# Attention outputs stored as two halves and added in the gating step, in a two-layer streaming encoder

## The chip, the cores and the metric

The kernel runs on one NeuronCore of a Trainium2 chip. Five engines work side by side: TensorE (PE) for matmuls, VectorE (DVE), ScalarE (ACT) and GpSimd (POOL) for element-wise work, and SyncE (SP), which here issues every DMA. Matmuls write to PSUM; the other operands lie in SBUF; the large intermediates go through DRAM. The metric is the device time of one execution in microseconds (us), the median of several runs.

## The reference

The program is one inference step of two encoder layers for 2048 prompt tokens and 32 sample tokens, with d_model 1024. What matters here is layer 0: two attention branches from one projection, each gated, concatenated and sent through one output projection.

```python
qa, ka, va, ga, qb, kb, vb, gb = ab_project(hp, pos_p, w_in_ab[j])
oa = prompt_band(qa, ka, va, N_PREV_A, None, sinks_a[j])      # 8 query heads, 2 KV heads, window 2 chunks, sinks
ob = prompt_band(qb, kb, vb, N_PREV_B, relpos_b[j], None)     # 8 heads, window 8 chunks, bias table
mp = ab_output(oa, ob, ga, gb, w_out_ab[j])

def ab_output(oa, ob, ga, gb, w_out):
    y = jnp.concatenate([oa.reshape(b, t, -1) * jax.nn.silu(ga),
                         ob.reshape(b, t, -1) * jax.nn.silu(gb)], axis=-1)
    return y @ w_out
```

Layer 1 is a gated linear recurrence (projection, width-4 convolution, gates, scan, output projection). Everything is fp32.

## The kernel before, in words

**Precision.** A matrix product in fp32 is made of fast products of a high and a low part: each operand is split into h (rounded) and l (the rest), and three matmuls h·h, h·l, l·h are summed in PSUM (`mm_list`, L819). So every weight tile is split (`w_split`, L484: the copy h on ACT or DVE, the difference l on DVE or POOL), and every activation block too (`r0h`, `r0l`). In the attention the values v lie as 64 high and 64 low columns side by side, so one matmul gives 128 PSUM rows: rows 0 to 63 from the high part of v, rows 64 to 127 from its low part. Their sum is the attention output of a head.

**Stages.** Tokens are cut into three blocks b of about 700, each in two halves bi of 352 (the last 324). `dense_P` (L1126) runs the 26 column tiles of the input projection for b = 0, 1, 2. As soon as q, k and v of a block have been written to DRAM, the attention units of that block start. `dense_2` (L1954) then runs the output projection (`out_part`) of the three blocks, and layer 1 block by block.

**One attention unit** (`soft`, L1231, and `transp`, `evac_O`, `evac_B`). PE makes the scores S. `reduce` (L1242) runs one custom DVE operation per PSUM tile: it adds bias or mask, writes the negated scores to `pt` and their row minimum to `nm`. Branch B has its keys in two PSUM tiles, so two operations give two minima, and a third small operation `nm<-nm` (L1257) joins them. ACT takes the exponential with the row sum; DVE takes the reciprocal `rr`; DVE or POOL scales `pt` by `rr` and by 0.5 (the 0.5 belongs to the gate, which is stored as twice its SiLU). PE transposes the result into T; ACT and DVE split T into the two parts `pp`. PE multiplies by v into O.

**Evacuation of O.** `evac_O` (branch A, four heads side by side, 512 columns) lets ACT copy one 64-row half of O to the tile `ot`, and DVE add the other half. `evac_B` (branch B) has 512 columns in which the high and low part of the scores lie beside each other too, so that a second DVE operation adds `ot` to `ot` over 256 columns. One DMA then writes 64 rows to oT in DRAM, which has 1024 rows, one per output feature.

**Gating.** `y_proc` (L784) loads oT and the gate zT in pieces of 4 feature tiles by 176 tokens, multiplies them, and splits the product into `r0h`/`r0l` (or `r1h`/`r1l`), the operand of the output projection. For block 0 it starts near the end of `dense_P`, and writes over `r0` once `dense_P` no longer reads it.

**What sets the order.** The instructions of every engine are put in order while the program is built, by a list scheduler (`Sched`): each step is a small process that waits for its inputs and buffers, states its cost on each engine it may use, and gets the engine that would end first. PE never waits in that plan: matmuls of the dense parts, four at a time (`CHK`), fill what the attention leaves free. After the attention `sch.alone` keeps POOL out of such choices. On the chip each engine runs its list strictly in that order, and waits on semaphores. So a change of a cost or a step moves instructions in all lists.

## Time and profile before

| what | value |
|---|---|
| median of 3 runs | 1827.37 us (1827.22 to 1828.31) |
| the profiled execution | 1823.5 us |
| its span, first to last instruction | 1821.7 us |
| mean granted TensorE clock | 0.988 |
| DMA, moved | 362.80 MB, mean 199 GB/s |
| attention, first and last O matmul start | 95.3 us, about 1002 us |

The profile was taken by the hardware profiler on one execution. Nearly every instruction is issued through one helper, so that all rows have the line L101; groups are told apart by the tiles that they write and read, written as out<-in. "CUSTOM_DVE_ANT_0 pt<-S,bias" is the operation of `reduce`, and "DVE_READ_ACCUMULATOR2_ANT nm" the read of its minimum. A row of a group gives its count after x, then busy time and mean ns of one, then the idle time of the engine just before them with what ended it. A row of the stages gives start:end, length, and for each engine its busy us, then the granted clock, the DMA share and GB/s. Records of one matmul are longer than the distance between two starts, because matmuls overlap.

### The profile page before, as it was taken

How to read it: one execution, taken by the hardware profiler on the slowest of the kernel's cores; microseconds unless marked ns; L12 is line 12 of the kernel's file. 1: busy time of each engine (PE TensorE's matmuls, PEld its weight loads, DVE VectorE, ACT ScalarE, POOL GpSimd, SP SyncE). 2: the span in 40 equal slices, each digit the busy share in tenths (PEclk: the TensorE clock that was granted, in tenths of full speed). 3: DMA queues.
4: the chain of work that ended last, by engine and by line, in shares of the span. 5: the costliest groups of instructions: out<-in, count | busy, mean ns of one | idle time of the engine just before them, and what ended most of it. 6: DMA issues, size and time to landing. Idle time of an engine off the chain costs nothing.

```text
span 1821.7 us, 31694 instructions
## 1 busy us (share of the span) xinstructions
PE 1731.5 (95%) x11078; PEld 1671.8 (92%) x11078; DVE 1555.3 (85%) x3330; ACT 996.5 (55%) x2037; POOL 326.5 (18%) x284
## 2 busy tenths in 40 slices
PE   8999999999999999999998999998999999999995
PEld 7999999998999999899997999998999899999995
DVE  9899967899998779998988789899999988798843
ACT  4275543476666416665565344457753675447831
POOL 4332204323322233311222000000011000100002
PEclk8999999999999999999998999999999999999998
DMA  5788766888654368877764985684566735575376
GB/s 179 203 245 265 228 190 196 226 232 237 192 149 141 97 186 248 210 217 195 216 194 122 278 248 168 210 267 147 217 213 217 204 124 174 165 208 171 128 268 193
DMA packets 293576, 362.80 MB, mean 199 GB/s; under 512 B 36308, under 2 KB 244616, under 8 KB 293400
## 3 DMA queue, kind: packets, MB, share of 16 engines
q1 hardware_dynamic: 293416, 360.78, 66.5%
q8 instruction: 87, 1.43, 0.3%
q14 instruction: 73, 0.60, 0.1%
HBM read 255.77 MB, written 107.00 MB: 199 GB/s over the span
## 4 chain that ended last, share of the span: by engine, by line
PE 49%; DVE 29%; DMA 9%; ACT 6%; issue 4%; SPq 1%; POOL 1%; DVEq 0%; ACTq 0%; POOLq 0%
PE acc L101 35%; PE T L101 4%; PE O L101 4%; PE S L101 4%; DVE pt L101 3%; DVE ex L101 3%; DVE m L101 3%; DMA xr<-x2T 3%; DVE ss L101 2%; DVE ti L101 2%; DVE xs L101 2%; DVE s L101 2%; DVE pp L101 2%; DVE eti L101 1%; DVE wl L101 1%
## 5 line engine op out<-in xcount | busy, mean ns | idle before, releaser
L101 PE MATMUL acc<-r0h,wh 128*128 128x352 f32 (+2 forms) x1832 | 592.1, 323 | 6.7 <-ACT tzb L101 2.9
L101 PE MATMUL acc<-r0h,wl 128*128 128x352 f32 (+2 forms) x1832 | 592.2, 323 | 2.9 <-DMA wl<-wo1s 2.9
L101 PE MATMUL acc<-r0l,wh 128*128 128x352 f32 (+2 forms) x1832 | 592.5, 323 | 0.6 <-DVE r0l L101 0.5
L101 PEld LDWEIGHTS acc<-r0h,wh 128*128 128x128 f32 x1832 | 346.2, 189 | 9.3 <-ACT tzb L101 3.1
L101 PEld LDWEIGHTS acc<-r0h,wl 128*128 128x128 f32 x1832 | 346.3, 189 | 4.8 <-DMA wl<-wo1s 4.0
L101 PEld LDWEIGHTS acc<-r0l,wh 128*128 128x128 f32 x1832 | 346.4, 189 | 2.2 <-DVE r0l L101 1.2
L101 PE MATMUL acc<-r1h,wh 128*128 128x352 f32 (+1 forms) x864 | 277.5, 321 | 5.2 <-ACT tz L101 3.6
L101 PE MATMUL acc<-r1h,wl 128*128 128x352 f32 (+1 forms) x864 | 277.0, 321 | 1.6 <-DVE wl L101 1.6
L101 PE MATMUL acc<-r1l,wh 128*128 128x352 f32 (+1 forms) x864 | 276.9, 321 | 0.0
L101 ACT ACTIVATE pt<-pt,nm 128x256 f32<-128x256 f32 (+6 forms) x272 | 169.8, 627 | 61.2 <-DVE nm L101 59.3
L101 ACT CAST pp<-T 128x256 fp32r<-128x256 f32 (+4 forms) x314 | 134.0, 438 | 84.3 <-PE T L101 65.8
L101 PEld LDWEIGHTS acc<-r1h,wh 128*128 128x128 f32 x864 | 162.3, 188 | 6.4 <-ACT tz L101 4.5
L101 POOL TENSOR_SCALAR pt<-pt,rr 128x256 f32<-128x256 f32 (+4 forms) x142 | 100.2, 716 | 366.4 <-DVE rr L101 217.0
L101 PEld LDWEIGHTS acc<-r1h,wl 128*128 128x128 f32 x864 | 162.3, 188 | 1.9 <-DVE wl L101 1.9
L101 PEld LDWEIGHTS acc<-r1l,wh 128*128 128x128 f32 x864 | 162.3, 188 | 0.0
L101 PE MATMUL T<-ident,pt 128*128 128x128 f32 (+2 forms) x864 | 143.3, 274 | 18.0 <-DVE pp L101 10.2
L101 DVE TENSOR_TENSOR pp<-T,pp 128x256 fp32r<-128x256 f32 (+4 forms) x314 | 150.4, 496 | 7.9 <-ACT pp L101 6.0
L101 PE MATMUL O<-pp,vt 128*128 128x256 f32 (+3 forms) x728 | 135.9, 310 | 9.8 <-DVE pp L101 4.7
L101 PEld LDWEIGHTS T<-ident,pt 128*128 128x128 f32 (+2 forms) x864 | 101.7, 140 | 42.4 <-DVE pp L101 19.9
L101 DVE CUSTOM_DVE_ANT_0 pt<-S,bias 128x320 f32<-128x320 f32 (+2 forms) x240 | 108.8, 478 | 17.4 <-PE S L101 14.6
L101 PE MATMUL S<-kk,qa 128*128 128x320 f32 (+5 forms) x376 | 119.7, 333 | 3.8 <-DVE nm L101 3.3
L101 PEld LDWEIGHTS O<-pp,vt 128*128 128x128 f32 (+1 forms) x728 | 107.1, 193 | 16.0 <-DVE pp L101 6.1
(241 smaller groups left out, 3010.1 us busy)
## 6 DMA issues: line engine op xcount, KB each, us to landing
wst<-w_in SPq DMA_DIRECT2D x93, 512.0 KB, 4.4
wst<-wo_in SPq DMA_DIRECT2D x32, 512.0 KB, 5.6
wh<-w1s SPq DMA_DIRECT2D x32, 512.0 KB, 3.8
wl<-w1s SPq DMA_DIRECT2D x32, 512.0 KB, 4.6
wh<-wo1s SPq DMA_DIRECT2D x24, 512.0 KB, 3.9
wl<-wo1s SPq DMA_DIRECT2D x24, 512.0 KB, 4.7
kk<-kB SPq DMA_DIRECT2D x32, 320.0 KB, 4.8
vt<-vB SPq DMA_DIRECT2D x16, 640.0 KB, 4.8
```

What stands on the lines that cost most here:

```text
L101: r = fn(*a, **k)
```

## The change

- oT gets 2048 rows. For each head the sums from the high and from the low half of v are both kept; they are added when the gating step reads them.
- Branch A (`evac_O`): two ACT copies of 128 rows by 256 columns and two DMAs; no DVE operation. The ring `ot` is four tiles of 256 columns instead of four half-tiles of 512.
- Branch B and the sample units (`evac_add`): ACT copies one 256-column part over all 128 rows, DVE adds the other part; the second DVE addition is gone.
- `y_proc`: pieces of 2 feature tiles by 352 tokens. Two DMAs bring the high rows and the low rows, z comes in one tile for two pieces. One more addition per piece, then product, copy and difference as before. The readiness of the operand is told for each feature tile (`(key, bi, c)`), no longer for the whole half.
- `reduce`: the minimum of the first PSUM tile is the start value of the second operation, and the small `nm<-nm` is gone.
- The scaling of `pt` may go to ACT for branch B (units with one row of `out`), and no longer has the factor 0.5; the 24 weight tiles of the output projection are multiplied by 0.5 in `w_split` instead, where their difference l is now always on DVE.

```diff
-    oT, zT, x2T = dt("oT", [D, TOK]), dt("zT", [D, TOK]), dt("x2T", [D, TOK])
+    oT, zT, x2T = dt("oT", [2 * D, TOK]), dt("zT", [D, TOK]), dt("x2T", [D, TOK])
...
+            half = WSEQ[i][0] == "wo0"
+            if half:
+                if e == "A":
+                    A.activation(h, s, AF.Copy, scale=0.5)
+                else:
+                    V.tensor_scalar(h, s, 0.5, None, OP.mult)
+                yield R("V", [h])
+                V.scalar_tensor_tensor(l, s, 0.5, f32(h), OP.mult, OP.subtract)
...
     def y_proc(b, ri, key, free=None, then=None):
-        todo = [(bi, t0, col, w, 4 * j) for bi, t0, col, w in cells_of(b) for j in range(2)]
+        todo = [(bi, T0[2 * b + bi], BW[2 * b + bi], k) for bi in range(2) for k in range(0, KT, 2)]
...
+                if k % 4 == 0:
+                    g = xrr if b == 0 else xtr
+                    z, = yield R("SP", [("z", b)], [g])
+                    SP.dma_start(out=tile4(z)[:, :, :w], in_=zT[k * 128:k * 128 + 512, t0:t0 + w].rearrange("(k p) t -> p k t", p=128))
+                x, = yield R("SP", [("o", min(b + 1, 2))], [xtr])
+                for j in range(2):
+                    r = k * 256 + j * 256
+                    SP.dma_start(out=tile4(x)[j * 64:j * 64 + 64, :, :w], in_=oT[r:r + 256, t0:t0 + w].rearrange("(s d) t -> d s t", s=4))
...
-            ENG[e].tensor_tensor(o, o, x[:, 4:8, :w], OP.mult)
+            ENG[e].tensor_tensor(o, o, v[:, :, 1], OP.add)
+            e, _ = yield R(("V", "G"), [lambda: th, z], cost=(0.8, 1.63))
+            ENG[e].tensor_tensor(o, o, tile4(z)[:, k % 4:k % 4 + 2, :w], OP.mult)
...
-            if n % 4 == 3:
-                sch.set((key, bi), max(sch.t["V"], sch.t["G"]) + 0.13)
+            for c in range(k, k + 2):
+                sch.set((key, bi, c), sch.t[e] + 0.13)
...
-    otr = Ring(sch, ap, [128, 512], F32, "ot", 2, halves=True)
+    otr = ring(ap, [128, 256], "ot", 4)
...
-        def reduce(ps, pieces, o0):
-            yield R("V", [ps] + ex)
+        def reduce(ps, pieces, o0, gi):
+            on = gi > 0 and sink is None
+            yield R("V", [ps] + ex + ([(uid, 0)] if on else []))
...
-                                       scalar=BIG if sink is None else nsk[:np_, sink + j:sink + j + 1],
+                                       scalar=nsk[:np_, sink + j:sink + j + 1] if sink is not None else nm[:np_, 1:2] if on else BIG,
...
-                if sink is None and len(groups) == 2:
-                    V.tensor_tensor(nm[:np_, 0:1], nm[:np_, 0:1], nm[:np_, 1:2], OP.min)
...
-        e, _ = yield R(("V", "G"), [r], cost=(0.06 + n * 0.00053, 0.1 + n * 0.00106))
+        e, _ = yield R(("V", "G", "A")[:3 if len(out) == 1 else 2], [r], cost=(0.06 + n * 0.00053, 0.1 + n * 0.00106, 0.197 + n / 1200.0))
...
-            ENG[e].tensor_scalar(x, x, r[:np_, j:j + 1], 0.5, OP.mult, OP.mult)
+            if e == "A":
+                A.activation(x, x, AF.Copy, scale=r[:np_, j:j + 1])
+            else:
+                ENG[e].tensor_scalar(x, x, r[:np_, j:j + 1], None, OP.mult)
...
+    def evac_O(b, ps, g, t0):
+        for i in range(2):
+            ot, = yield R("A", [ps], [otr])
+            A.copy(ot, ps[:, i * 256:i * 256 + 256])
+            if i:
+                Or.release(ps)
+            yield R("SP", [ot])
+            SP.dma_start(out=o_two(g, i, t0, 128), in_=ot.rearrange("p (j n) -> p j n", j=2))
+            otr.release(ot)
+        o_done(b)
...
+    def evac_add(b, ps, v0, v1, dsts, i0=None):
...
+            A.copy(o2[:, i0:], v0[:, i0:])
+            if i0:
+                A.copy(o2[:, 0], v1[:, 0])
+            yield R("V", [ot])
+            V.tensor_tensor(o2[:, i0:], v1[:, i0:], o2[:, i0:], OP.add)
         Or.release(ps)
...
-    def evac_B(b, ps, dst, i0):
-        A.copy(o[:, i0:], v[64 - x:128 - x, i0:])
-        V.tensor_tensor(o[:, i0:], v[x:x + 64, i0:], o[:, i0:], OP.add)
-        V.tensor_tensor(o[:, i0:, 1], o[:, i0:, 0], o[:, i0:, 1], OP.add)
-        SP.dma_start(out=dst, in_=ot[:, 256:512])
```

All lists move. Three places are shown; the numbers behind a tile's name tell its buffers apart.

The first place is DVE in the last attention units of branch B, where O is emptied (`ot`), T is split (`pp`) and the minimum is taken (`pt`, `nm`). Before:

```order
L101 TENSOR_TENSOR ot_215<-O_198,ot_215 64x2x2x128
L101 TENSOR_TENSOR pp_213<-T_196,pp_213 128x3x128
L101 ISA pt_211,nm_218<-S_194,bias_208 128x320
L101 ISA nm_218 128x1
L101 TENSOR_TENSOR ot_215<-ot_215 64x256
L101 TENSOR_TENSOR pp_213<-T_197,pp_213 128x2x128
L101 ISA pt_211,nm_218<-S_195,bias_208 128x320
L101 ISA nm_218 128x1
L101 TENSOR_TENSOR nm_218<-nm_218 128x1
```

and now:

```order
L101 ISA pt_209,nm_218<-S_194,bias_208 128x320
L101 ISA nm_218 128x1
L101 ISA pt_209,nm_218<-S_195,bias_208,nm_218 128x320
L101 ISA nm_218 128x1
L101 TENSOR_TENSOR pp_213<-T_196,pp_213 32x32
L101 TENSOR_TENSOR ot_216<-O_198,ot_216 128x256
```

The join `nm<-nm` and the addition `ot<-ot` are gone, the addition of O has 256 columns over 128 rows, and the second custom operation reads `nm`.

The second place is DVE where the attention ends and the operand of the first output projection (`r0l`, from `xt`) is made. Before, this is mixed with attention units:

```order
L101 TENSOR_TENSOR xt_152<-xt_152 128x704
L101 TENSOR_TENSOR pp_212<-T_196,pp_212 128x4x32
L101 TENSOR_TENSOR ot_214<-O_198,ot_214 64x2x2x128
L101 ISA pt_210,nm_217<-S_194,bias_207 32x272
L101 ISA nm_217 32x1
L101 TENSOR_TENSOR r0l<-xt_152,r0h 128x4x176
```

and now it stands behind the last split `pp` of the attention, between weight splits (`wh`, `wl`) and the last gates (`s`):

```order
L101 TENSOR_TENSOR pp_213<-T_197,pp_213 128x2x128
L101 TENSOR_TENSOR r0l<-xt_151,r0h 128x2x352
L101 TENSOR_TENSOR r0l<-xt_152,r0h 128x2x352
L101 TENSOR_TENSOR ot_215<-O_198,ot_215 128x256
L101 SCALAR_TENSOR_TENSOR s_187<-s_187,acc_158 128x352
L101 TENSOR_SCALAR wh_119<-wst_117 128x1024
L101 SCALAR_TENSOR_TENSOR wl_122<-wst_117,wh_119 128x1024
L101 SCALAR_TENSOR_TENSOR s_182<-s_182,acc_159 128x324
L101 TENSOR_TENSOR xt_151<-xt_151 128x2x352
L101 TENSOR_SCALAR wh_120<-wst_118 128x1024
L101 TENSOR_TENSOR xt_151<-xt_151,xr_153 128x2x352
```

So the gating of block 0 moved from the attention's last units to behind them.

The third place is PE at the last O matmuls. Before, what follows is the output projection (352 columns, block 0):

```order
L101 MATMUL O_198<-pp_212,vt_206 128x2x128 x8
L101 MATMUL O_198<-pp_212,vt_206 128x256 x2
L101 MATMUL acc_159<-r0h,wl_123 128x352
L101 MATMUL acc_159<-r0h,wh_120 128x352
L101 MATMUL acc_159<-r0l,wh_120 128x352
```

and now it is the end of the input projection (the 324 columns are the last half of block 2; the last O matmul stands one row above):

```order
L101 MATMUL acc_158<-r0h,wh_121 128x352
L101 MATMUL acc_158<-r0l,wh_121 128x352
L101 MATMUL acc_158<-r0h,wl_124 128x352
L101 MATMUL acc_159<-r0h,wh_119 128x324
L101 MATMUL acc_159<-r0l,wh_119 128x324
L101 MATMUL acc_159<-r0h,wl_122 128x324
```

What filled PE inside the attention now follows it. Counted over the whole list of PE, 168 dense matmuls moved from ahead of the last O matmul to behind it: between it and the first matmul on `r1` there are now 460 dense matmuls, where there were 292. 76 of them still belong to the input projection. The number of matmuls is the same, 11061. Over the whole list of DVE there are 3183 instructions, where there were 3332, on ACT 1836 (1767), on POOL 199 (289), and on SP 1274 (1227); of the 142 scalings of `pt` on POOL 69 are left, 44 stand on ACT (none before), and DVE has 159 (130).

More of the change, by code (lines that the diff above doesn't have):

```diff
@@ L566, in late_consts @@
         V.tensor_scalar(nsk, sk, -1.0, None, OP.mult)
-        SP.dma_start(out=oT[:, SEQ:S0].rearrange("(k p) t -> p k t", p=128), in_=zpad)
+        for x in range(2):
+            SP.dma_start(out=oT[x * D:(x + 1) * D, SEQ:S0].rearrange("(k p) t -> p k t", p=128), in_=zpad)
         V.tensor_scalar(hba, vec[:, BA], 0.5, None, OP.mult)
@@ L1410, in proc @@
                 run.v_done(2)
[L1411 removed]
+                yield from evac_add(b, po, out[:, :, 0], out[:, :, 1], [o_head(8 + h, ta * 128, 256)], 2 - len(edges))
             return proc
@@ L1509, in proc @@
             run.v_done()
-            yield from evac_O(2, po, 128, oT[g * 256:(g + 1) * 256, S0:TOK].rearrange("(j d) n -> d j n", j=4),
-                              lambda ot: ot[:, :128].rearrange("d (j n) -> d j n", j=4), True)
+            yield from evac_add(2, po, po[:, 128:256], po[:, :128], [o_two(g, i, S0, DEC) for i in range(2)])
         return Run(with_cache(need(2, (0, 1, 3 + 2 * g))),
```

96 lines of the change are left out of this document (47 added, 49 removed).

## The prediction

> **What bounds the kernel now.** I read the busy shares first, then a table by stage, then what PE waited for, then the chain that ended last.
>
> ```profile
> PE 1731.5 (95%) x11078; PEld 1671.8 (92%) x11078; DVE 1555.3 (85%) x3330; ACT 996.5 (55%) x2037; POOL 326.5 (18%) x284
> q1 hardware_dynamic: 293416, 360.78, 66.5%
> 95.00:300.00 205.00, 199.76 (x1291) 192.78 (x1290) 175.82 (x441) 114.93 (x291) 48.91 (x50) 1.00 0.77 225
> 300.00:350.00 50.00, 48.14 (x306) 47.13 (x305) 40.10 (x74) 14.56 (x41) 19.18 (x17) 1.00 0.75 214
> 350.00:600.00 250.00, 239.53 (x1611) 226.14 (x1611) 234.11 (x687) 166.90 (x403) 73.29 (x70) 0.99 0.68 189
> 600.00:700.00 100.00, 98.72 (x653) 97.29 (x652) 73.51 (x149) 34.74 (x83) 30.86 (x26) 1.00 0.60 174
> 700.00:955.00 255.00, 247.79 (x1714) 234.30 (x1713) 230.21 (x717) 161.63 (x413) 62.45 (x61) 1.00 0.76 208
> 955.00:1003.00 48.00, 41.32 (x259) 38.34 (x258) 38.21 (x98) 24.94 (x58) 14.96 (x9) 0.89 0.43 126
> 1003.00:1190.00 187.00, 178.38 (x1112) 176.69 (x1111) 157.44 (x219) 80.92 (x144) 0.94 (x1) 0.99 0.78 229
> 975.00:980.00 5.00, 3.92 (x18) 3.30 (x18) 4.62 (x13) 2.55 (x8) 0.00 (x0) 0.53 0.22 68
> 980.00:985.00 5.00, 4.83 (x21) 3.97 (x22) 2.84 (x12) 1.94 (x6) 0.00 (x0) 0.50 0.27 71
> ```
>
> PE bounds the whole, so a saving elsewhere can only return time in which PE stands still. In the attention, 95 to 1003, PE is busy 199.8 + 48.1 + 239.5 + 98.7 + 247.8 + 41.3 = 875.2 of 908 us: 32.8 us idle, 6.7 of them in the last 48. There the clock also falls to half for 10 us, which costs some 5 us more. About 38 us of visible loss, then, is what the change can win here. DVE is busy 792 of the same 908 us, and 464 of 505 us in the two rows of dense attention (350 to 600, 700 to 955). What does PE wait for, from 50 to 950?
>
> ```profile
> PE T L101 <- DVE pp L101: 6.9, 12, 2.1
> PE O L101 <- DVE pp L101: 3.2, 4, 1.1
> PE O L101 <- DVE ot L101: 2.7, 2, 2.0
> PE S L101 <- DVE nm L101: 2.7, 3, 1.1
> ```
>
> These waits, the four largest, all end on DVE. In the tail, the chain of waits (start, length, what) shows why:
>
> ```profile
> 949.45 5.53 DMA xt<-zT
> 955.08 1.84 DVE xt L101
> 958.18 1.75 DVE nm L101
> 969.98 2.39 POOL wl L101
> 1001.11 1.19 PE O L101 x10
> ```
>
> The gating of block 0 (`xt`, with its load of zT), a weight split on POOL and the 128x1 join `nm` stand on the chain while the last attention units still run. The last O matmuls start at 1001.
>
> **The change, part by part.** The groups of DVE by shape, then of POOL and ACT, that carry the prices:
>
> ```profile
> L101 DVE TENSOR_TENSOR ot<-O,ot 64x512 f32<-64x512 f32 x80 | 54.9, 686 | 11.2 <-ACT ot L101 10.0
> L101 DVE TENSOR_TENSOR ot<-ot 64x256 f32<-64x256 f32 x48 | 24.4, 507 | 0.8
> L101 DVE TENSOR_TENSOR ot<-O,ot 64x256 f32<-64x256 f32 x18 | 7.5, 417 | 1.8 <-ACT ot L101 1.4
> L101 DVE TENSOR_TENSOR nm<-nm 128x1 f32<-128x1 f32 x96 | 30.8, 321 | 3.3
> L101 DVE TENSOR_TENSOR nm<-nm x104: 147/159/1815, 412.8 to 989.9; 128x1 f32<-128x1 f32 x96, 32x1 f32<-32x1 f32 x8
> L101 DVE TENSOR_TENSOR pp<-T,pp 128x256 fp32r<-128x256 f32 x104 | 42.2, 415 | 1.8 <-ACT pp L101 0.9
> L101 DVE CUSTOM_DVE_ANT_0 pt<-S,amask,nsk 128x256 f32<-128x256 f32 x120 | 51.6, 477 | 2.9 <-PE S L101 2.5
> L101 DVE CUSTOM_DVE_ANT_0 pt<-S,bias 128x256 f32<-128x256 f32 x8 | 3.3, 414 | 0.0
> L101 DVE TENSOR_SCALAR pt<-pt,rr 128x256 f32<-128x256 f32 x54 | 23.6, 492 | 0.2
> L101 DVE TENSOR_SCALAR pt<-pt,rr 128x640 f32<-128x640 f32 x39 | 24.5, 633 | 0.7
> L101 DVE TENSOR_TENSOR xt<-xt 128x704 f32<-128x704 f32 x11 | 10.7, 972 | 0.9 <-DMA xt<-zT 0.9
> L101 DVE TENSOR_TENSOR wl<-wst,wh 128x1024 fp32r<-128x1024 f32 x86 | 110.8, 1288 | 2.8 <-ACT wh L101 0.8
> L101 POOL TENSOR_TENSOR wl<-wst,wh 128x1024 fp32r<-128x1024 f32 x39 | 94.8, 2430 | 131.1 <-ACT wh L101 90.3 <-PE S L101 14.2 <-PE O L101 8.8
> L101 POOL TENSOR_SCALAR pt<-pt,rr 128x640 f32<-128x640 f32 x57 | 55.2, 970 | 237.1 <-DVE rr L101 146.1 <-ACT pp L101 39.0 <-PE O L101 13.3
> L101 ACT ACTIVATE pt<-pt,nm 128x640 f32<-128x640 f32 x96 | 79.9, 832 | 37.4 <-DVE nm L101 35.8 <-DVE pp L101 1.2
> L101 ACT COPY ot<-O 64x512 f32<-64x512 f32 x80 | 46.5, 581 | 47.7 <-PE O L101 45.1 <-DMA bvs_out<-s 1.3
> L101 ACT CAST pp<-T 128x256 fp32r<-128x256 f32 x104 | 38.4, 372 | 27.4 <-PE T L101 19.8 <-DVE rr L101 4.1 <-DVE nm L101 0.8
> ```
>
> *Evacuation.* Half the rows never made an addition cheaper: 64x512 takes 686 ns. Removed from DVE: 54.9 + 24.4 + 7.5 = 86.8 us. Added: 48 additions of 128x256 out of PSUM, as `pp<-T,pp`, 48 x 0.415 = 19.9 us; the 18 of half that size at most 18 x 0.415 = 7.5. Net 59 us.
>
> *Minimum.* 96 joins go, 30.8 us. A start value read from a tile costs 477 - 414 = 63 ns by the two custom rows, 96 x 0.063 = 6. Net 25 us. The second operation must follow the first, but both already stood in that order on one engine.
>
> *Scaling of `pt`.* 73 go from POOL, 44 to ACT and 29 to DVE. On DVE that is 29 x 0.49 = 14 us more. ACT has no row of this; its nearest is the exponential of 640, 832 ns: some 44 x 0.83 = 37 us more, less 80 x 0.581 - 112 x 0.372 = 5 us from the copies of O. ACT is busy 55%, which covers that; uncovered, in front of a `pp` copy that PE waits for, it would cost up to those 32 us. On POOL a scaling took 970 ns, so no unit's latency grows.
>
> The Trainium skill, ScalarE: Activation LUTs, Rules for kernel authors, speaks against this part: it sends multiplications to VectorE. By its rule these scalings would cost 0.63 us each by the DVE row, against 0.83 on ACT. The trace decides here by load, not by rate: DVE is the loaded engine.
>
> *Attention, sum.* DVE loses 59 + 25 - 14 = 70 of 792 us, 9%, and the gating of block 0 leaves the tail. What PE gets back lies between 0 and the 38 us that are visible. Of the tail's 6.7 + 5 us I take 9, since what stood on its chain is now behind the attention or gone. Of the other 26 I take 11, more than 9%, since waits of this kind come in bunches where DVE is late. **Gain 20 us.**
>
> *Behind the attention.* The 168 moved matmuls cost PE nothing in sum. But POOL is shut out there, and DVE gets: 24 additions of a piece (24 x 0.97 = 23 us), the product and difference of block 0's eight pieces, so far inside the attention (16 x 0.97 = 16), and ten weight differences from POOL (10 x 1.29 = 13). To the 157 of 187 us that makes 209 us. PE's work there grows by 168 at the dense pace:
>
> ```profile
> 1003.00:1056.00 53.00, 53.00 (x335) 53.00 (x334) 39.51 (x53) 21.47 (x39) 0.94 (x1) 1.00 0.88 267
> ```
>
> 53 / 335 = 0.158 us, so 26.6 us, to 187 + 27 = 214 us. DVE thus goes from 84% to 98% of the stage and will now and then be late for PE. Nothing at best; at worst the rival below. **Loss 6 us.**
>
> *DMA.* oT doubles: 1024 more rows of 2084 fp32 values, 8.5 MB, are written and read, 17 of 361 MB. The queue's packets take 66.5% of the engines' time, so this hides; 47 more issues on SP stand mostly ahead of loads that have time. I take nothing; the hole priced below contains a late load.
>
> *Sum.* -20 + 6 = -14 us. The profiled execution took 1823.5 us (span 1821.7), 4 us under the median; the same step from the median 1827.4 gives **1813 us**.
>
> **Rivals.**
>
> *Nothing returns.* The plan puts fewer fillers into the attention, so units follow each other as tightly for the lighter DVE as before, and its waits stay per unit. For it: 168 fillers left the attention. Against it: four large PE waits all end on DVE, and the join takes 321 ns with a median of 159. Gain and loss then cancel: 6 - 6, 1827.
>
> *A hole at the hand-over, and a DVE-bound stage behind it.* `y_proc` may write `r0` only when `dense_P` stops reading it, and now nothing of the attention is left to fill. From there DVE must do 20 operations of a piece and three weight differences, 19.4 + 3.9 = 23 us, before the second half's operand is complete, and some eight smaller ones at about 0.45, 27 in all. PE has 76 matmuls and two groups of 24, 124 x 0.158 = 20 us. The hole is 4 to 7 us; as the rows at 975 and 980 show, the clock may then halve for 10 us, 5 more. With DVE late by another 12 us in the rest of that stage (it has 5 us to spare in 214) that is 24 us against a gain which, in this case, I put at 12: 1827 + 12 = 1839. It decides once the stage's loss passes the attention's gain.
>
> *All of it returns, and more.* A matmul's record is longer than the pace at which matmuls start, so short waits don't show as idle. With all 38 us back and no loss behind: 1827 - 38 = 1789. For it: the join's longest row is 1815 ns, its shortest 147, and while such rows stretch, POOL is at work (`wl` at 969.98); 90 instructions leave POOL.
>
> The Trainium skill, GPSIMD Engine Reference, Specifications, says that POOL shares its SBUF interfaces with VectorE and collides with DVE operations that read two SBUF inputs or use both ports. The stretched joins agree. By that rule the remaining DVE operations get faster too, which this rival contains.
>
> *The change doesn't do what it says*: the list shows the joins and the second additions gone, so only a delay elsewhere could hide it; this is the first rival.
>
> **How the numbers follow.** The forecast, 1803 to 1822, gets 0.58. Nothing returns, 1822 to 1832: 0.13. The hole, 1832 to 1845: 0.16. All returns, 1785 to 1803: 0.13. The range 1797 to 1834 leaves out the far ends of the last two. A change of 0.2%, 3.7 us, is about what a measurement of this kernel can tell from none. Faster by more: 0.58 + 0.13, and 0.01 of the first rival, 0.72; within it 0.10; slower 0.18, the hole and 0.02 of the first rival.
>
> **What would show it.** In the profile after: DVE some 70 us lighter ahead of the last O matmul, which comes about 40 us earlier (27 us of moved fillers and most of the gain); PE's waits for `pp`, `ot` and `nm` smaller; no clock dip ahead of it. Behind it DVE at 95% and more, and a PE wait for `r0l` or `r0h` of a few us. Wrong: PE idle ahead of the last O matmul as before, PE waits for ACT `pp` in place of DVE's, or a hole of 10 us and a half clock at the first output projection.

## The result and the profile after

The changed kernel takes 1882.4 us (median of 4 runs, 1881.1 to 1886.6), against 1827.8 us for the kernel before (4 runs, 1827.2 to 1833.9): a ratio of 1.030, 95% interval 1.028 to 1.032. It is slower by 55 us where 14 less were forecast. The profiled execution took 1883.0 us, its span is 1881.2 us, and the mean granted clock fell from 0.988 to 0.969.

First the busy shares and the packets' queue of the kernel after, with the stages cut as in the prediction (columns: start:end, length, then PE, weight load, DVE, ACT, POOL, granted clock, DMA share, GB/s):

```profile
PE 1753.9 (93%) x11078; PEld 1687.6 (90%) x11078; DVE 1506.3 (80%) x3181; ACT 1000.1 (53%) x2106; POOL 279.1 (15%) x194
q1 hardware_dynamic: 302360, 377.85, 69.3%
95.00:300.00 205.00, 197.86 (x1275) 190.19 (x1275) 161.44 (x412) 109.35 (x296) 39.59 (x31) 1.00 0.77 230
300.00:350.00 50.00, 48.32 (x304) 47.30 (x303) 39.23 (x70) 13.97 (x37) 17.50 (x16) 1.00 0.79 217
350.00:600.00 250.00, 243.01 (x1646) 228.28 (x1647) 224.60 (x659) 169.92 (x438) 64.10 (x38) 1.00 0.74 204
600.00:700.00 100.00, 97.62 (x638) 96.54 (x638) 68.39 (x133) 30.54 (x75) 31.31 (x24) 1.00 0.63 180
700.00:920.00 220.00, 212.65 (x1451) 198.35 (x1451) 177.18 (x577) 149.04 (x405) 35.96 (x26) 0.99 0.81 217
920.00:969.00 49.00, 47.46 (x340) 45.17 (x339) 37.88 (x123) 30.99 (x79) 9.97 (x5) 1.00 0.60 170
969.00:1215.00 246.00, 214.08 (x1258) 207.87 (x1257) 188.22 (x254) 92.33 (x163) 0.00 (x0) 0.92 0.87 227
```

The attention, 95 to 969, lost its dip: the clock is 1.00 ahead of the last O. DVE is busy 161.4 + 39.2 + 224.6 + 68.4 + 177.2 + 37.9 = 709 us there, 83 less than before's 792. PE is still idle 874 - 846.9 = 27 us, so most of the 32.8 us stayed. In the last row the clock falls to 0.92 and PE stands for 32 us.

To place the loss I cut both traces at four events: the last O matmul, the first store of x2T (the output projection's first result) and the first stores of yT of layer 1's first and second block. Since 168 dense matmuls moved from ahead of the last O to behind it, 168 x 0.158 = 26.5 us are put back in A and taken off in B. The group of O matmuls (the fifth and sixth numbers are its first start and last) and the stores, before and then after:

```profile
L101 PE MATMUL O<-pp,vt x728: 193/283/582, 95.3 to 1002.0; 128*128 128x256 f32 x141, 128*128 128x512 f32 x31, 128*128 128x64 f32 x8, 32*128 32x64 f32 x2
1061.60 0.36 SPq L101 DMA_DIRECT2D x2T<-m  x1
1405.15 0.39 SPq L101 DMA_DIRECT2D yT_out<-m  x1
1611.48 0.39 SPq L101 DMA_DIRECT2D yT_out<-m  x1
```

```profile
L101 PE MATMUL O<-pp,vt x728: 192/283/561, 94.0 to 968.3; 128*128 128x256 f32 x139, 128*128 128x512 f32 x31, 128*128 128x64 f32 x8, 32*128 32x64 f32 x4
1086.84 0.38 SPq L101 DMA_DIRECT2D x2T<-m  x1
1435.63 0.39 SPq L101 DMA_DIRECT2D yT_out<-m  x1
1663.41 0.39 SPq L101 DMA_DIRECT2D yT_out<-m  x1
```

| stage | before | after | difference |
|---|---|---|---|
| A: first to last O, corrected | 906.7 | 874.3 + 26.5 = 900.8 | -5.9 |
| B: last O to first x2T store, corrected | 59.6 | 118.5 - 26.5 = 92.0 | +32.4 |
| C: to the first yT store | 343.6 | 348.8 | +5.2 |
| D: to the first yT store of the second block | 206.3 | 227.8 | +21.5 |
| E: to the end of the span | 210.2 | 217.8 | +7.6 |

So the attention won 6 of the 20 us forecast, and two holes cost 54 us. Eight runs, this one among them, have the same order in the attention and the same POOL instructions; their A lies between -4.6 and -10.6, so a difference of 4 us in A says little.

**The first hole, 980 to 1020.** The windows there, in the kernel after:

```profile
980.00:990.00 10.00, 4.62 (x26) 3.79 (x24) 5.56 (x8) 2.17 (x3) 0.00 (x0) 0.89 1.03 238
990.00:1000.00 10.00, 0.00 (x0) 0.00 (x0) 0.43 (x1) 1.45 (x3) 0.00 (x0) 0.50 1.09 247
1000.00:1010.00 10.00, 7.49 (x18) 5.01 (x18) 7.76 (x9) 1.94 (x4) 0.00 (x0) 0.50 0.81 217
1010.00:1020.00 10.00, 9.17 (x44) 8.80 (x45) 7.35 (x9) 3.90 (x7) 0.00 (x0) 0.74 0.76 197
```

In 40 us 88 matmuls run; at 0.158 us there would be 253, so 165 x 0.158 = 26 us are lost here. All 16 DMA engines are full (share 1.03 to 1.09), and yet move only 238 to 247 GB/s. What PE waits for from 975 to 1020, and what ACT and DVE do (start, duration; in brackets the idle time before and its releaser):

```profile
PE acc L101 <- ACT r0h L101: 16.9, 4, 14.8
998.55 0.55 ACT L101 ACTIVATE m<-acc,vec 128x352 f32<-128x352 f32 x1 [15.45 <-DMA zT<-s]
999.34 0.78 ACT L101 CAST r0h<-ex 128x704 fp32r<-128x704 f32 x1
988.62 0.89 DVE L101 TENSOR_TENSOR ex<-ex 128x704 f32<-128x704 f32 x1 [4.40 <-DMA ex<-oT]
989.54 0.89 DVE L101 TENSOR_TENSOR ex<-ex,eti 128x704 f32<-128x704 f32 x1
1000.15 0.89 DVE L101 TENSOR_TENSOR r0l<-ex,r0h 128x704 fp32r<-128x704 f32 x1 [9.72 <-ACT r0h L101]
```

The product of the next piece is done at 990.4, but its cast to `r0h` starts only at 999.3: ahead of it in ACT's list stands the first write of `m`, which waited 15.45 us for a store of zT out of `s`. `m` lies in memory in which `s` lay before, so its first write needs that store to have landed. PE waits 14.8 us for the cast. And DVE waited 4.4 us for the load of oT.

**The second hole, in D,** lies at layer 1's change of blocks (window of 40 us, then PE's largest wait there):

```profile
1420.00:1460.00 40.00, 21.91 (x124) 21.00 (x124) 35.51 (x59) 9.36 (x14) 0.00 (x0) 0.79 0.53 140
PE acc L101 <- ACT r1h L101: 16.7, 1, 16.7
```

PE waits 16.7 us for the next block's operand while DVE is busy 35.5 of 40 us. The diff has no edit in layer 1; only the plan's result differs there.

### The profile page after: what moved, and what is told of

The parts are those of the page before. It is cut to its first block, busy times and chain, and to the rows that moved or that the text cites. A ratio compares the mean times of both kernels' runs of the same rounds, so it can differ in the third digit from the quotient of the medians.

```text
span 1881.2 us, 31507 instructions
## 1 busy us (share of the span) xinstructions
PE 1753.9 (93%) x11078; PEld 1687.6 (90%) x11078; DVE 1506.3 (80%) x3181; ACT 1000.1 (53%) x2106; POOL 279.1 (15%) x194
## 5 line engine op out<-in xcount | busy, mean ns | idle before, releaser
L101 PE MATMUL acc<-r1h,wh 128*128 128x352 f32 (+1 forms) x864 | 281.0, 325 | 19.8 <-ACT r1h L101 16.7
L101 ACT CAST pp<-T 128x256 fp32r<-128x256 f32 (+5 forms) x314 | 133.6, 438 | 86.1 <-PE T L101 81.5
L101 DVE TENSOR_TENSOR pp<-T,pp 128x256 fp32r<-128x256 f32 (+5 forms) x314 | 149.9, 499 | 20.9 <-ACT pp L101 20.7
L101 POOL TENSOR_TENSOR wl<-wst,wh 128x1024 fp32r<-128x1024 f32 x29 | 70.4, 2426 | 607.2 <-DVE wh L101 513.8
L101 PE MATMUL T<-ident,pt 128*128 128x128 f32 (+2 forms) x864 | 144.6, 275 | 13.4 <-POOL pt L101 9.1
L101 PE MATMUL O<-pp,vt 128*128 128x256 f32 (+2 forms) x728 | 132.6, 307 | 9.4 <-ACT ot L101 3.7
L101 POOL TENSOR_SCALAR pt<-pt,rr 128x256 f32<-128x256 f32 (+6 forms) x69 | 87.0, 1270 | 326.7 <-DVE rr L101 129.3
L101 ACT ACTIVATE m<-acc,vec 128x352 f32<-128x352 f32 (+2 forms) x89 | 48.7, 547 | 144.5 <-PE acc L101 128.5
```

Source lines behind the costliest of these rows:

```text
L101: r = fn(*a, **k)
```

## The experiments

All medians beside those of the kernel before on the same chip (1825 to 1828 us). A to E are differences to before as in the table above, from each run's profile; their sum differs from the difference of the spans by the start of the first O (within 1.3 us). Each run's correction uses its own count of moved matmuls.

| run | us | ratio, 95% interval | A | B | C | D | E |
|---|---|---|---|---|---|---|---|
| after | 1882.4 | 1.0301 [1.0281, 1.0321] | -5.9 | +32.4 | +5.2 | +21.5 | +7.6 |
| e1_norm_first | 1854.5 | 1.0158 [1.0135, 1.0181] | -6.5 | +31.0 | +6.7 | -4.0 | +3.7 |
| e2_before_cost | 1846.3 | 1.0118 [1.0093, 1.0142] | +0.3 | 0.0 | +0.9 | +22.3 | -4.0 |
| e3_m_swap | 1870.6 | 1.0247 [1.0226, 1.0269] | -6.2 | +27.3 | +4.0 | +21.0 | +1.1 |
| e4_halves_alone | 1860.9 | 1.0188 [1.0167, 1.0209] | -8.4 | +33.0 | +13.5 | -1.7 | +3.5 |
| e5_both | 1853.6 | 1.0138 [1.0107, 1.0168] | -8.2 | +26.4 | +8.0 | -5.1 | +4.7 |
| e6_no_halves | 1835.3 | 1.0048 [1.0029, 1.0066] | +2.0 | +4.5 | +3.6 | -0.1 | +1.0 |
| e7_half_loads | 1836.2 | 1.0055 [1.0037, 1.0073] | -5.4 | +13.7 | +6.0 | -5.3 | +2.6 |
| e8_no_additions | 1853.1 | 1.0126 [1.0091, 1.0161] | -4.6 | +27.1 | +10.8 | -5.0 | +6.3 |
| e9_wide_permuted | 1836.2 | 1.0042 [1.0020, 1.0063] | -10.6 | +13.7 | +5.9 | -5.5 | +3.2 |
| e10_wide | 1864.1 | 1.0221 [1.0178, 1.0264] | +8.3 | +14.7 | +7.8 | -0.7 | +6.8 |
| e11_scale_no_pool | 1852.7 | 1.0147 [1.0108, 1.0186] | -11.3 | +32.9 | +11.1 | -0.8 | +2.0 |
| e12_wide_rows | 1835.2 | 1.0053 [1.0032, 1.0074] | -6.6 | +14.2 | +6.7 | -5.6 | -0.7 |
| e13_dense_first | 1832.0 | 1.0039 [1.0024, 1.0054] | -3.4 | +10.8 | -0.5 | -0.7 | +2.1 |
| e14_pool_two_ops | 1827.9 | 1.0017 [1.0004, 1.0031] | -14.7 | +14.6 | +3.9 | -4.3 | +4.5 |
| e15_two_ops_dense_first | 1826.5 | 1.0000 [0.9988, 1.0012] | -10.7 | +10.7 | +0.8 | -0.3 | +1.5 |
| e16_no_halves_two_ops | 1832.4 | 1.0033 [1.0019, 1.0047] | -1.0 | +5.2 | +2.9 | +0.6 | -1.3 |
| e17_norm_order | 1827.5 | 0.9996 [0.9980, 1.0011] | -8.7 | +14.3 | +0.7 | -0.4 | +4.2 |
| e18_scale_three | 1824.8 | 0.9992 [0.9977, 1.0006] | -14.9 | +8.2 | -1.7 | -0.6 | +8.4 |

### The order of layer 1, the tile m, and the halves alone

**e1_norm_first** gives the normalisation of layer 1's next block priority in the plan.

```diff
-PY2, PY3 = 0.5, 3
+PY2, PY3 = 0.5, -0.5
```

> The changed kernel, with one number of the list scheduler different: the norm of layer 1's next block (PY3) goes ahead of the output projection's closing work instead of behind it. All engines' lists are the same, instruction by instruction, until that norm is placed, near 1300 us of the profile; then only their order differs. Theory A (the 16.7 us wait of PE for r1h near 1430 to 1450, with its half clock, is an accident of the order that the re-planned lists took there, and no cost of the new instructions): that wait goes, and the time falls by 20 to 27 us, to 1855 to 1862. Theory B (DVE and DMA are really too loaded behind the attention, so that the lost time only shows there): the wait moves to another place and the time falls by less than 8 us. Hand-over hole near 985 to 1015 unchanged in both.

D fell from +21.5 to -4.0, and the time by 28 us. The same window as above, now in e1:

```profile
1420.00:1460.00 40.00, 39.43 (x243) 38.33 (x242) 37.59 (x56) 15.22 (x22) 1.93 (x2) 1.00 0.69 206
```

243 matmuls where 124 stood, and the clock at 1.00.

**e2_before_cost** changes one cost of the plan in the kernel before. No step of the program changes; the lists differ in their order and in a few choices of engine.

```diff
-PEM, VPT = 0.6, 0.06
+PEM, VPT = 0.6, 0.07
```

> The kernel before, with one assumed cost of the list scheduler changed (VPT 0.06 to 0.07 us, a scalar operand on DVE, used only behind the attention). No instruction of the kernel is added or removed apart from a few choices between engines. Theory A (the hole at layer 1's change of blocks is a matter of the order of the lists): the same wait of PE for r1h of some 15 to 20 us appears in the kernel before, and it gets 18 to 28 us slower, 1845 to 1856. Theory B (the hole comes from the changed instructions): within 5 us of the kernel before.

Without any part of the change, D grows by 22.3 us, with the same wait (e2, PE's waits at that place):

```profile
PE acc L101 <- ACT r1h L101: 16.4, 1, 16.4
```

The second hole is thus an accident of the plan, which a re-planned list falls into or not; the two runs show it from both sides.

**e3_m_swap** takes the two `m` tiles in the opposite order.

```diff
+    mr.idle = [(0.0, 1 - i, t) for _, i, t in mr.idle]
```

> The changed kernel, with the two tiles m of the output projection used in the opposite order. The lists are the same, only the memory of the first m is another: it no longer lies on the staging tiles s, from which the last store of zT is still read. Theory A (the hand-over hole is set by ACT, which waits 15.45 us for that store before its first write of m, with the casts r0h queued behind it): the first r0h behind it starts when its DVE product is done, 8.9 us earlier; the hole shrinks by 7 to 10 us and the time falls by 7 to 12, to 1870 to 1875. Theory B (the hole is set by the loads of oT or by DVE's 20 operations): the casts wait for DVE instead and the time falls by less than 3 us.

The write of `m` in e3 no longer waits for a store:

```profile
985.73 0.56 ACT L101 ACTIVATE m<-acc,vec 128x352 f32<-128x352 f32 x1 [2.28 <-PE acc L101]
990.33 0.78 ACT L101 CAST r0h<-ex 128x704 fp32r<-128x704 f32 x1 [3.69 <-DVE ex L101]
```

The cast starts 9 us earlier, the time falls by 12 us, but B only by 5: behind the removed wait stands the next one, for the load of oT (DVE, e3):

```profile
988.48 0.89 DVE L101 TENSOR_TENSOR ex<-ex 128x704 f32<-128x704 f32 x1 [3.91 <-DMA ex<-oT]
```

**e4_halves_alone**: the kernel before with the stores of O, the sums in `evac_add` and the gating of the change; minimum and scaling as before.

> The kernel before with one part of the change alone: the two halves of O in oT, added in the gating step; the minimum is joined by its own operation, and pt is scaled with 0.5 on DVE or POOL as before. Theory A (the hand-over is what the halves cost: the attention ends before the gating of block 0 is through, so nothing covers it): a wait of PE for r0h or r0l of 15 to 25 us in all near 985 to 1015 with half clock; no hole near 1430, since the list that this version gets has none there; 1845 to 1862. Theory B (it takes the joined minimum or the scaling on ACT to open the hand-over hole): below 1835.

B is +33, so the halves alone make the first hole. The second isn't there; C is +13.5, with a wait of PE of 12.8 us (for DVE's `xs`) that the kernel after doesn't have; another re-planned list, e10's, has one of 12.7.

### What the first hole consists of

**e5_both** joins the edits of e1 and e3; it is the base of the next runs.

> The changed kernel with both edits: the norm of layer 1's next block first (PY3), and the two tiles m used in the opposite order. Theory A (the two losses are separate, each worth what it was alone): 1882.4 less 27.9 less 11.8, 1839 to 1847. Theory B (the gain of one hides in the other): above 1850.

The sum of the two gains would give 1882.4 - 27.9 - 11.8 = 1842.7, and 1853.6 came. By the stages B fell by 4.6 from e1, as from the kernel after to e3 (5.1): the tile `m` is worth some 5 us at that place, and the other 7 of e3's 12 were in later stages (E above all) and didn't repeat. In the whole time the swap shows no clear gain here: e5's median is 0.9 us below e1's, and the intervals of their ratios overlap.

**e6_no_halves** is the other side of e4: the kernel before with the joined minimum, the scaling on three engines (0.5 moved into the weights) and e3's edit, O stored as before.

> The kernel before with the joined minimum and the scaling on ACT (0.5 in the weights), but without the two halves: oT, its evacuation and the gating as before; the tiles m in the opposite order, so that no wait for the store of zT is mixed in. Theory A (only the halves open the hole at the hand-over, by what they add behind the attention): PE waits for r0h and r0l by less than 4 us there and the time is below 1820. Theory B (any version whose attention ends before the gating of block 0 is through has the hole, since nothing else fills PE there): a PE wait for r0h of 8 to 14 us right behind the last O matmul, with half clock, the attention's gain given back, and 1820 to 1840.

The hole is nearly gone (+4.5, against +26.4 in e5, which also has `m` swapped), and PE's wait for `r0h` there is 3.1 us: theory A has the place right. But the gain in the attention is gone too (+2.0), and so the time lies where B put it. PE's largest wait in the attention of e6, where before had 1.4 us for `pt` by POOL:

```profile
PE T L101 <- POOL pt L101: 13.0, 21, 1.7
```

**e7_half_loads** is e5 with each load bringing only the rows from the high part of v; the addition reads them twice, so the low sums are left out.

```diff
-                    SP.dma_start(out=tile4(x)[j * 64:j * 64 + 64, :, :w], in_=oT[r:r + 256, t0:t0 + w]...)
+                    nc.sync.dma_start(out=xo...[:, :, 0], in_=xi...[:, :, 0])
```

> As the changed kernel with both edits, in the same order of instructions, but each load of oT brings the high rows alone; the addition reads the high rows twice. What is left out: the low rows' 8.5 MB of loads and their part in the result. Theory A (at the hand-over DVE waits for the loads of oT, with 3.9 and 2.2 us, because the DMA engines are full from 970 to 1100): these waits shrink, and the time falls by 6 to 12 us below the version with both edits. Theory B (the chain of DVE and ACT operations sets the hole, the loads only fill its gaps): less than 3 us.

17.4 us less than e5, 12.7 of them in B: the loads' landing is part of the hole.

**e8_no_additions** is e5 without the 24 additions of the gating, so the low sums are loaded but not used.

```diff
-            ENG[e].tensor_tensor(o, o, v[:, :, 1], OP.add)
```

> As the changed kernel with both edits, in the same order, but the 24 additions of the gating step are left out, so that the result holds the high rows' part alone; all loads are as they were. Theory A (the loads set the hole): less than 3 us faster than the version with both edits. Theory B (DVE's chain at the hand-over and DVE's load in the output projections set the time): four pieces of 0.92 us shorter at the hand-over and some more behind it, 5 to 12 us faster.

0.5 us less, and B no smaller: behind the narrow loads the additions cost nothing, since DVE then only waits longer for the loads of oT (13.4 us from 968 to 1020, where e5 had 10.7). What they cost once the loads are faster, no run shows.

**e9_wide_permuted** is e5 with every load of the same 352 KB going into 128 partitions instead of 64; the same rows land in another place, so that the addition pairs other rows.

```diff
-   out=tile4(x)[j * 64:j * 64 + 64, :, :w], in_=oT[r:r + 256, t0:t0 + w].rearrange("(s d) t -> d s t", s=4)
+   out=tile4(x)[:, 2 * j:2 * j + 2, :w],    in_=oT[r:r + 256, t0:t0 + w].rearrange("(s p) t -> p s t", p=128)
```

> As the changed kernel with both edits, in the same order, with as many loads of the same size; only, each of the two loads of a piece fills two of the tile's four columns over all 128 partitions, where the changed kernel fills all four over 64 partitions. What is changed in the result: rows of heads and of high and low parts land permuted. Theory A (a load into 64 partitions keeps the DMA engines busy longer per byte: from 985 to 1000 and from 1030 to 1050 they moved 223 to 255 GB/s at a share of 1.05 to 1.09, in the kernel before 295 to 357 at the same share): the loads of oT land in 4 to 6.5 us in place of 7 to 9, a full share moves over 300 GB/s, and the time falls by 7 to 16 us to 1838 to 1847. The Trainium skill, SBUF - State Buffer, Door 1: The DMA port swizzle, says that partitions 0 to 63 reach only half of the DMA ports; theory A is what that rule would do here. Theory B (what counts is the doubled number of bytes and loads): within 4 us of the version with both edits.

17.4 us less, as e7, with all the bytes moved: into 128 partitions the whole amount costs B no more than half of it does into 64. The loads issued from 970 to 1100 (count, KB each, median us from issue to landing) and the packets' queue, in the kernel after:

```profile
ex<-oT SPq DMA_DIRECT2D x20, 352.0 KB, 7.8
xt<-oT SPq DMA_DIRECT2D x14, 352.0 KB, 8.1
q1 hardware_dynamic: 23574, 31.11, 97.5%
```

and in e9:

```profile
ex<-oT SPq DMA_DIRECT2D x20, 352.0 KB, 6.3
xt<-oT SPq DMA_DIRECT2D x12, 352.0 KB, 5.7
q1 hardware_dynamic: 29567, 37.56, 89.9%
```

More bytes move in e9 (37.6 against 31.1 MB) with the engines less full. The Trainium skill, SBUF — State Buffer, Door 1: The DMA port swizzle (why `[64,N]` ≈ `[32,N]`), says that a transfer's rate depends on how many of the 16 ports to SBUF its partitions reach, and that partitions 0 to 63 reach half of them, as 64 to 127 do. The traces agree: 237 to 250 GB/s at a full share from 985 to 1000 in the kernel after, 362 to 397 from 980 to 995 in e9, and there in the last 5 us:

```profile
990.00:995.00 5.00, 3.68 (x11) 2.39 (x9) 3.57 (x5) 1.25 (x2) 0.00 (x0) 0.50 1.04 397
```

**e10_wide** loads as e9 and makes up for it in the stores: each O tile leaves in two stores of 64 partitions, 146 stores more, and the plan is made anew.

> The same with the reference's result: the rows of oT lie such that 128 partitions load 128 rows in sequence, and each store of an O tile is cut into two of 64 partitions, 146 more stores in all, in the attention. The lists are planned anew. Theory A: the gain at the hand-over stays, the stores are covered by the attention, 1836 to 1848. Theory B (the stores, now twice as many and from 64 partitions each, hold the last pieces back): the first store of x2T comes as late as without it, and the time is above 1850.

B stays good (+14.7), but the attention loses what that won: A is +8.3, 16.5 more than in e5. Part of it are loads of the queries, which stand behind the stores in SP's list and for which PE now waits; the rest isn't taken apart, since the plan differs too:

```profile
PE S L101 <- DMA qa<-qB: 6.9, 3, 4.3
```

**e12_wide_rows** reaches the same without more stores: in oT the rows of two heads alternate, so that a wide load puts each row where the sum wants it. The gate's columns and the rows of the output weights take the same order beforehand. The order on the engines is that of e5.

```diff
-        r = (h // 4 * 4 + h % 2 * 2 + h % 4 // 2) * 128
-        return oT[r:r + 128, t0:t0 + w]
+        r = h // 2 * 256
+        return oT[r:r + 256, t0:t0 + w].rearrange("(p j) t -> p j t", j=2)[:, h % 2]
```

> The changed kernel with both edits and wide loads, with the reference's result, and without more stores: in oT the rows of a pair of heads alternate, so that a store still covers 128 partitions and a load does too; the rows of the output weights and the gate's columns are laid out in the same alternating order beforehand. Instructions and order as in the version with both edits. Theory A (the narrow loads are the whole of the DMA's part): as with the permuted wide loads, 1832 to 1840, and the attention as long as without them, 871 to 876 us from the first to the last O matmul. Theory B (what the cut stores cost, 15 us in the attention, is a cost of any layout for wide loads): above 1845.

1835.2 us, B +14.2. With `m` and the loads put right, 14 us of the hole remain. In the windows from 980 to 1005 of e12, 68 matmuls run where 158 would at 0.158 us, which is these 14 us. What DVE and ACT do meanwhile, in order of time (the last row closes the fourth piece):

```profile
986.17 0.89 DVE L101 TENSOR_TENSOR ex<-ex 128x704 f32<-128x704 f32 x1 [1.80 <-DMA ex<-oT]
987.10 0.89 DVE L101 TENSOR_TENSOR ex<-ex,eti 128x704 f32<-128x704 f32 x1
988.03 0.78 ACT L101 CAST r0h<-ex 128x704 fp32r<-128x704 f32 x1 [1.58 <-DVE ex L101]
988.84 0.89 DVE L101 TENSOR_TENSOR r0l<-ex,r0h 128x704 fp32r<-128x704 f32 x1 [0.84 <-ACT r0h L101]
989.65 0.88 DVE L101 TENSOR_TENSOR ex<-ex 128x704 f32<-128x704 f32 x1
999.23 0.89 DVE L101 TENSOR_TENSOR r0l<-xt,r0h 128x704 fp32r<-128x704 f32 x1 [0.84 <-ACT r0h L101]
```

Once the first load has landed, sum, product, cast on ACT and difference follow one another, 3.5 us a piece, and four pieces take from 986.2 to 1000.1. The chain of e12 that ended last runs through them, and no other wait for a load stands in between.

**e13_dense_first** asks whether those 14 are missing cover: from column tile 23 of the last block `dense_P` goes ahead of the attention, so that the attention's last units are left for the hand-over (60 matmuls moved instead of 168).

```diff
+                if b == 2 and c == 23 and bi == 0:
+                    sch.reprio('dense_P', -5)
```

> The same with two changes in the order: from column tile 23 of the last block on, the dense projection goes ahead of the attention, so that the attention's last units stand behind it (108 dense matmuls more ahead of the last O matmul); and VPT 0.05, which acts only behind the attention. Theory A (what is left of the hand-over hole, some 14 us with the half clock, is the missing cover: nothing but the attention can fill PE while block 0 is gated): the hole near 975 to 1010 shrinks by 4 to 8 us, and with 3 to 6 us less waiting in layer 1 the time is 1820 to 1832, level with the kernel before or up to 0.3% faster. Theory B (units moved behind the dense projection wait for the same DVE and leave the same hole): above 1834.

A + B is +7.4, against +7.6 in e12: the hole is 3.4 us smaller and the attention 3.2 longer, which is within the spread of A. The time is 3.2 us lower, but the intervals of the ratios overlap and the spans of the two profiles are equal (1829.2 and 1829.3), so no stage can be named for it. More cover, made in this way, brought nothing that shows. What is left of the hole goes with the chain of the four pieces, while the clock stands at half; no run shortens that chain behind wide loads, so that it sets these 14 us is read from the trace and not shown by an experiment.

### What the attention didn't give back

**e11_scale_no_pool** is e5 with branch B's scaling on DVE and ACT only.

```diff
-        e, _ = yield R(("V", "G", "A")[:3 if len(out) == 1 else 2], [r], ...)
+        e, _ = yield R(("V", "A") if len(out) == 1 else ("V", "G"), [r], ...)
```

> The changed kernel with both edits, with the scaling of pt of branch B on DVE or ACT alone, never on POOL. Theory A (in the attention, POOL's scalings of about 1 us took over from DVE's waits: PE waits for pt from POOL 9.1 us, 15 times, where it was 1.4): this wait goes and the attention, at 158 ns for each matmul of the dense parts that stands ahead of its last O matmul, gets 4 to 9 us shorter. Theory B (units follow one another as tightly as the lists allow, so another wait takes its place): less than 2 us shorter. The whole time is not compared, since the lists behind differ too.

PE's wait for `pt` by POOL falls from 9.1 to 2.6 us; A is -11.3, 3.1 us better than e5 and some 4.5 better than the mean of the eight runs with the order of the kernel after. That lies between the theories or at the edge of theory A, and within the spread. But the row of POOL's scaling had changed. Before, it stands in the prediction with 970 ns; in the kernel after:

```profile
L101 POOL TENSOR_SCALAR pt<-pt,rr 128x640 f32<-128x640 f32 x17 | 34.1, 2008 | 175.3 <-ACT pt L101 57.7 <-PE T L101 34.0 <-DVE rr L101 25.9
L101 POOL TENSOR_SCALAR pt<-pt,rr 128x256 f32<-128x256 f32 x37 | 36.2, 993 | 42.2 <-DVE rr L101 34.4 <-ACT pt L101 7.5 <-ACT pp L101 0.4
```

The scaling by 0.5 went into the weights, and with it the second operation of the instruction. On POOL the shorter form takes 2008 / 970 = 2.07 times as long. The smaller shape in the kernel before:

```profile
L101 POOL TENSOR_SCALAR pt<-pt,rr 128x256 f32<-128x256 f32 x74 | 38.7, 542 | 66.6 <-DVE rr L101 21.6 <-ACT sr L101 13.0 <-PE O L101 8.4
```

**e14_pool_two_ops** is e12 with a second operation that does nothing, on POOL alone; every list is the same.

```diff
-                ENG[e].tensor_scalar(x, x, r[:np_, j:j + 1], None, OP.mult)
+                ENG[e].tensor_scalar(x, x, r[:np_, j:j + 1], *((1.0, OP.mult, OP.mult) if e == "G" else (None, OP.mult)))
```

> As the version with both edits and wide rows, in the same order; only the 69 scalings of pt on POOL multiply by rr and then by 1.0, as the kernel before multiplied by rr and by 0.5. Theory A (on POOL the form with one multiplication is slow: its 128x640 took 2008 ns after the change and 970 before, its 128x256 993 and 542): the 128x640 takes 0.9 to 1.05 us again, PE's wait for pt from POOL falls from 9 us to under 3, the attention from the first to the last O matmul gets 3 to 9 us shorter (873.6 without the edit), and the time falls to 1826 to 1833. Theory B (POOL's scalings are long because they run beside other DVE operations than before): they stay near 2 us and the time within 2 us.

```profile
L101 POOL TENSOR_SCALAR pt<-pt,rr 128x640 f32<-128x640 f32 x17 | 15.8, 931 | 192.5 <-ACT pt L101 60.2 <-DVE rr L101 57.8 <-PE T L101 37.2
```

931 ns, PE's wait for `pt` by POOL from 8.8 to 0.4 us, A from -6.6 to -14.7, and 7.3 us less in time: 1827.9 (6.6 by the ratios, whose intervals don't meet).

**e16_no_halves_two_ops** does the same to e6.

> The kernel before with the joined minimum, the scaling on ACT too and the tiles m swapped, without the halves, which took 1835.3 us; now with two multiplications in POOL's 111 scalings. Theory A (its attention lost 2 us, where fewer DVE operations should have won some, since POOL's scalings doubled): the attention gets 5 to 12 us shorter and the time falls to 1822 to 1831, at or below the kernel before. Theory B (the joined minimum and the scaling on ACT bring nothing even so): within 3 us of 1835.

2.9 us less, A -1.0. Minimum and scaling alone, even with the fast form, bring the attention nothing beyond the spread; PE waits 13.2 us for DVE's `pp` there. So the halves are needed for what e14's attention won, alone (e4's A is -8.4) or together with the rest.

### Versions to beat both

**e15_two_ops_dense_first** is e13 with e14's edit, **e17_norm_order** e14 with `VPT` 0.07, **e18_scale_three** e14 with the scaling open to three engines in both branches and `VPT` 0.05.

> The same with the dense projection first from column tile 23 on and VPT 0.05. Theory A: 3 to 8 us below the 1832.0 that this order took with the slow form, 1824 to 1829, level with the kernel before. Theory B: within 2 us of 1832.

> The repaired change (norm first, tiles m swapped, wide rows, two multiplications on POOL; 1827.9 us) with VPT 0.07: the order differs from 1180 us on only, ahead of that nothing changes. Theory A (the waits of PE for xs near 1260 to 1280, some 5 to 9 us with the slowed clock, are again a matter of order): they get 3 to 8 us smaller and the time is 1820 to 1826. Theory B (DVE is full there in any order, 96 of 100 us from 1200 to 1300): within 2.5 us of 1827.9.

> The repaired change with the scaling of pt open to DVE, POOL and ACT in both branches, and VPT 0.05. All lists are planned anew; more of the attention stands at the hand-over (112 dense matmuls more ahead of the last O matmul). Theory A (with the slow form, the narrow loads and the order's hole gone, the lighter DVE is worth what the attention gained, some 14 us, less a hand-over loss of 7 to 10): 1818 to 1826, faster than the kernel before. Theory B (the hand-over takes it all, however the attention is loaded): 1826 to 1834.

All three are level with the kernel before, e15 5.5 us below e13 as its theory A had it, e17 where e14 was, as its theory B had it; e18's 0.9992 has an interval that holds 1. e17 has e14's order in the attention and yet A is -8.7 against -14.7, so part of e14's A is the spread of single runs. No version was shown to be faster: in each, the attention's gain of 9 to 15 us meets a hand-over of 8 to 14 and a tail (E) of 2 to 8.

## Why the prediction was wrong

**Four steps of the sum failed.** One is a term that isn't in it: the sum stops behind the output projection and so puts layer 1 at nothing, without a reason, although the lists of all engines had moved. That was 21.5 us (the second hole, below).

The next is *DMA*: "so this hides ... I take nothing". I compared bytes and the engines' share, and not where the loads land nor when: each new load of oT goes into 64 partitions, and the rate at a full share is 237 to 250 GB/s, not 362 to 397. They are issued when `r0` waits for them. e9 shows 12.7 us of B in that alone. The 64 partitions stood in the diff, `tile4(x)[j * 64:j * 64 + 64]`, and I read past them.

The third is *Scaling of pt*: "On POOL a scaling took 970 ns, so no unit's latency grows". I took the price of an instruction with two operations for one with a single operation. It is 2008 ns, so each of the 17 tiles of 640 columns left on POOL took 1 us longer, and the 37 of 256 columns 0.45 us. Undoing it took 7.3 us off the time (e14). In A it was worth 8.1 us in e14 and 2.1 in e17, which has the same order there, so its size in A isn't firm.

The fourth is **the first hole**. It was a rival, and its place and its sign were right: PE waits for `r0h` with the clock at half, as the last sentence of the prediction has it for the case that it is wrong. Its price, 4 to 7 us and 5 for the clock, came out as 32. About 5 are ACT's wait for `m` (e3, e5) and 13 the narrow loads (e9); neither was priced, though *DMA* says that the hole contains a late load. For the remaining 14 the price set DVE's 23 us against PE's 20, as if DVE worked without a break from the moment that `r0` is free. The trace of e12 shows a chain instead that begins when the load has landed and changes between DVE and ACT, 3.5 us a piece, while PE stands waiting; as said, no run has tested it.

**The second hole**, 21.5 us, was in no case of mine, though I had the lists of both kernels. e1 and e2 show that it hangs on the plan and not on the changed instructions; that this plan fell into it was bad luck. The range could not hold such a jump: e2 alone moves the time by 1.2%.

**Attention, gain 20.** DVE's relief came out near the count: 83 us, against 70 plus the 16 of block 0's gating that went behind the last O. Two errors nearly cancel in it: the emptying of O (`ot`) fell by 74 us and not by 59, since the rows used leave out its smaller shapes, and 12 us of weight splits (`wh`, `wl`) moved into the attention. The clock's dip is gone as forecast, and the last O comes 34 us earlier, of which 27 are moved fillers. But only 6 came back, -10.6 to -4.6 over the runs of this order. PE's waits show why. Added up by the engine that ended them, DVE's fell from 25.5 us (95 to 1003, before) to 7.9 (95 to 969, after), nearly the gain that was forecast; but POOL's rose from 1.4 to 9.3 and ACT's from 0.3 to 4.0. Before, the largest was 10.2 for DVE's `pp`, and POOL's `pt` had 1.4; the three largest now:

```profile
PE T L101 <- POOL pt L101: 9.1, 15, 1.0
PE O L101 <- ACT ot L101: 3.7, 3, 2.0
PE T L101 <- DVE pp L101: 2.1, 7, 0.5
```

**The prices of single operations** held, read from these groups of the kernel after:

```profile
L101 ACT ACTIVATE pt<-pt,rr 128x640 f32<-128x640 f32 x37 | 30.7, 832 | 2.9 <-DVE rr L101 2.3
L101 DVE CUSTOM_DVE_ANT_0 pt<-S,bias,nm 128x320 f32<-128x320 f32 x96 | 52.8, 550 | 12.0 <-PE S L101 1.5 <-DVE nm L101 1.0 <-POOL pt L101 0.2
L101 DVE TENSOR_TENSOR ot<-O,ot 128x256 f32<-128x256 f32 x48 | 20.1, 419 | 8.4 <-ACT ot L101 7.9 <-DMA oT<-ot 0.4
```

ACT's scaling takes the 832 ns assumed, the sum of O 419 for 415, and the start value 550 - 487 = 63 ns, as priced (487 is the row without it in the same kernel). No run isolates the choice of ACT, so the rule of the Trainium skill on multiplications that the prediction weighed is neither borne out nor refuted here as a choice; one operation of 128x640 is longer on ACT (832 ns) than on DVE (662).

**Behind the attention, loss 6.** "DVE at 95% and more" was wrong: 188.2 of 246 us, 77%. DVE isn't the bound of the first part of this stage, where it waits for loads and for ACT, as PE does; only from 1150 to 1215 is it 94% busy. C and E, +5 and +8, are not taken apart.

**All of it returns** fell as well. Its reading of the joins was right: in the trace before, the 81 joins with no POOL operation beside them took at most 163 ns, the 23 with one 916 on average. But with the joins gone, the operations that remain on DVE aren't faster, although POOL runs 90 instructions less: `pp<-T,pp` of 128x256 took 415 ns before and 417 after. Beyond the joins, that sharing of POOL and DVE, for which the prediction cited the Trainium skill, gave no gain that these rows show.

## What to carry to other kernels

Before an operation is dropped from an instruction, or a transfer reshaped, look for a row of exactly that form: a shorter instruction may be the slower one, and a DMA share near 1 with 60% of the GB/s seen elsewhere is a reason to test the shape of the transfer. When work is taken from the end of one stage to the start of the next, list what the next stage's first operand needs (loads, memory that must come free, the instruction queued ahead) and price each as if nothing covered it, added up along the chain and not engine by engine. Where a planner sets the order, time a neutral change of one of its costs first: here that alone moved the time by 20 us, more than most of the parts.

## What the runs showed of the hardware

- POOL multiplies a 128x640 tile by a scalar per partition in 2008 ns with one operation in the instruction (kernel after), and in 970 (before) or 931 ns (e14) with two; 128x256 in 993 ns against 542.
- While loads of 352 KB into 64 partitions run, beside others, the DMA engines read as full (share 1.08 to 1.09) at 237 to 250 GB/s (kernel after, 985 to 1000); with the same loads into 128 partitions they moved 362 to 397 at a share of 1.03 to 1.07 (e9, 980 to 995).
- The granted clock was 0.50 in the 10 us without a matmul (990 to 1000 in the kernel after) and in the 10 us behind them, with 18 matmuls; in the next 10 us it was 0.74.
- A join on DVE (a minimum of two tiles of 128x1 or 32x1) took at most 163 ns with no POOL operation beside it, and up to 1815 ns with one (kernel before).
